# Modulation weights read in pieces of 256 rows by 512 columns, with their partial sums over 512 columns on VectorE alone

## The chip, the core and the metric

The kernel runs on one core of one Trainium2 chip. The metric is device time in microseconds (us), the median of several executions. Most executions of one kernel agree within 0.3%.

## The reference

One inference step of a four-layer network over 512 sample tokens and 128 prompt tokens, 1024 wide, all in float32. Every layer first makes its modulation vectors, normalises and modulates the tokens, runs a mixer of its kind (differential attention, retention, HGRN2, differential attention again), and adds the gated result to the tokens:

```
for l in range(DEPTH):                                   # 4 layers, kinds 0, 1, 2, 0
    sh_p, sc_p, ga_p = modulation(c_ctx[None, :], w_mod[l], b_mod[l])   # silu(c) @ w_mod[l] + b_mod[l],
    sh_s, sc_s, ga_s = modulation(c, w_mod[l], b_mod[l])                # cut into three parts of 1024
    hp = rms_norm(xp, g_pre[l]) * (1.0 + sc_p) + sh_p
    hs = rms_norm(xs, g_pre[l]) * (1.0 + sc_s) + sh_s
    yp, ys = mixer(hp), mixer(hs)                        # x @ w_in, the mixer, @ w_out
    xp = xp + ga_p * rms_norm(yp, g_post[l])
    xs = xs + ga_s * rms_norm(ys, g_post[l])
```

The change is in the product `silu(c) @ w_mod[l]`: a matrix of 1024 rows by 3072 columns per layer, against two vectors (the sample's c and the prompt's c_ctx). No value of the result is computed differently, apart from the order of the sums.

## The kernel before

**Work on TensorE.** All large products (x @ w_in, y @ w_out) are made of matmuls in fp32r, three for each product: the weights and the tokens are each cut into a high part (`whi`, `hh`) and a low part (`wlo`, `hl`). ScalarE makes the high part, VectorE (at line 116) the low part as a difference. TensorE's order is written out by hand (`manual_schedule`), by generators that `weave` interleaves: the projections of the next head fill the gaps of the mixer of this head. The order on VectorE, ScalarE, GpSimd and the DMA queue of SyncE (SP) is made by a scheduler that takes an instruction when its operands are ready by its own reckoning, so work that stands late in the program can be put into an earlier stage.

**The start** (`start`, lines 1270 to 1368). The first layer's shift and scale are made by TensorE, 128 columns at a time. Step k of 8: a product with `mraw` (line 1296), a copy `row` to SBUF (line 1298), a transposition on TensorE (line 1303), a reduction `mcol` (line 1305) and two small operations that write `modT` (lines 1306 and 1308). With `modT` the tokens, transposed on TensorE (line 1313), become `h` (line 1316), `hh` and `hl`, and then the first projection uses them (lines 1325 to 1327). All of it but TensorE's part, `hh` and `whi` runs on VectorE, in one queue.

**The other modulation vectors** are made off TensorE. `mod_load` fetches a piece of w_mod of 512 rows by 256 columns into `mraw` (two buffers) as 4 groups of 128 rows. `mod_next` is called after each unit of the projections with a number of groups (`mod_pace`). For a group and each of the two vectors it takes mraw times a column of silu(c) (`smod`) and adds it to `macc`, at line 371 on VectorE, 256 columns at once; for the first group, and in the two attention layers for every second group, ScalarE makes the product (line 369, into `mpart` for the latter, which VectorE adds over 512 values at line 373). `mpart` lies in the attention layer's own pool (`mod_pool`), so it can't be written before the stage ahead has given up that memory. After 8 groups the sums over rows still lie across the 128 partitions; `mod_turn` transposes them on TensorE (line 339, 4 of 128x128) and VectorE reduces them into `modT` (line 343). The table `MOD_IN` says which blocks of columns are made during which layer: 12 blocks of 256 in layer 0, 24 in layer 1, none in layer 2, 4 in layer 3.

**A boundary of two layers** (`out_layer`, lines 601 to 629). For each of five tiles of 128 tokens: y @ w_out, a norm, and the new tokens `xt` (line 619, VectorE). `pre` takes the sum of squares (line 408, ScalarE), `ms` (line 394, VectorE), `rs` (line 401, GpSimd) and the scaled tokens `xh` (line 410, ScalarE); `turn` transposes `xh` on TensorE (line 419) and makes `h` in two steps (lines 421 and 422, VectorE), `hh` (line 446, ScalarE) and `hl` (line 116, GpSimd for three of the tiles). The next layer's first products (`step`) use them. The chain xt, ms, rs, xh of the last tile is followed by a transposition at a fixed place in TensorE's order.

Of the kernel before, what the change touches and what calls it, by code (L numbers as in the profile page):

```python
# [11 lines left out]
F32 = mybir.dt.float32  # L12
# [3 lines left out]
AF = mybir.ActivationFunctionType  # L16
# [5 lines left out]
P = 128  # L22
# [15 lines left out]
         ("g", 3), ("qk", 7))  # L38
RW = (3.5, 9.0, 11.0, 0.5)
PACE = (155.0, 245.0, 195.0)  # L40
MOD_IN = (((0, range(8, 12)), (1, range(8))), ((1, range(8, 12)), (2, range(8)), (2, range(8, 12)), (3, range(8))), (),
          ((3, range(8, 12)),))
TOK = (0, 128, 384, 512, 256)


# [43 lines left out]
class Net:  # L89
    def __init__(self, ctx, tc, t):  # L90
        self.ctx, self.tc, self.nc, self.t = ctx, tc, tc.nc, t
        pool = lambda name, **kw: ctx.enter_context(tc.tile_pool(name=name, **kw))
        self.cp = pool("cp", bufs=1)
        self.wp = pool("wp", bufs=2)
        self.mp = pool("mp", bufs=1)
        self.dp = pool("dp", bufs=1, space=DRAM)
        self.pp = pool("pp", bufs=1, space=PSUM)
        self.mods, self.modr, self.modp = {}, [], None
        self.mod_owed, self.mod_row = 0, 0
        self.held = None  # L100

# [217 lines left out]
    def mod_load(self):  # L319

        if self.modq:
            l, b, i = self.modq.pop(0)
            raw = self.wp.tile([P, 4, 256], F32, tag="mraw", bufs=2, name="mraw")
            self.nc.sync.dma_start(raw, self.t["w_mod"][l, i * 512:i * 512 + 512, b * 256:b * 256 + 256].rearrange("(k p) n -> p k n", p=P))
            self.modr.append((l, b, i, raw))

    def mod_turn(self):

        nc = self.nc
        if self.modp is None:  # L330
            return
        l, b, acc = self.modp
        self.modp = None
        if b == 0:
            self.mods[l] = self.cp.tile([P, 24, 2], F32, tag="modT", bufs=3, name="modT")
        ps = self.one([P, 2, 2, P])
        for c in range(2):
            for j in range(2):
                nc.tensor.transpose(ps[:, c, j, :], acc[:, j, c * 128:c * 128 + 128], self.ident)
        r = slice(2 * b, 2 * b + 2)  # L340
        m = self.mods[l][:, r, :]
        wide = lambda a: a.unsqueeze(2).to_broadcast([P, 2, 2])
        nc.vector.tensor_reduce(out=m, in_=ps, axis=AX.X, op=ALU.add)
        nc.vector.tensor_tensor(out=m, in0=m, in1=wide(self.bmodT[:, l, r]), op=ALU.add)
        if 4 <= b < 8:
            nc.vector.tensor_scalar(out=m, in0=m, scalar1=1.0, scalar2=None, op0=ALU.add)
        if b >= 4:
            g = (self.gpre if b < 8 else self.gpost)[:, l, b % 4 * 2:b % 4 * 2 + 2]
            nc.vector.tensor_tensor(out=m, in0=m, in1=wide(g), op=ALU.mult)

    def mod_next(self, rows):

        nc = self.nc
        self.mod_owed += rows
        while self.mod_owed >= 1 and self.modr:
            self.mod_owed -= 1
            l, b, i, raw = self.modr[0]
            k = self.mod_row
            first = i == k == 0
            if first:  # L360
                self.macc = self.mp.tile([P, 2, 256], F32, tag="macc", bufs=2, name="macc")
            part = self.macc if first else None
            pool = self.mod_pool if k % 2 else None
            if pool is not None:
                part = pool.tile([P, 2, 256], F32, tag="mpart", bufs=2, name="mpart")
            for j in range(2):
                m, c = self.macc[:, j, :], self.smod[:, 4 * i + k, j:j + 1]
                if part is not None:
                    nc.scalar.activation(part[:, j, :], raw[:, k, :], AF.Copy, scale=c)
                else:  # L370
                    nc.vector.scalar_tensor_tensor(out=m, in0=raw[:, k, :], scalar=c, in1=m, op0=ALU.mult, op1=ALU.add)  # L371
            if pool is not None:
                nc.vector.tensor_tensor(out=self.macc, in0=self.macc, in1=part, op=ALU.add)
            if 4 * i + k == 5:
                self.mod_turn()
            self.mod_row = (k + 1) % 4
            if k == 3:
                self.modr.pop(0)
                if i == 1:
                    self.modp = (l, b, self.macc)  # L380
                self.mod_load()

    def mod_finish(self):
        self.mod_next(200)
        self.mod_turn()
        self.mod_owed = 0

# [268 lines left out]
    def diff(self, l, y):  # L656
        nc, tc, t = self.nc, self.tc, self.t
        j = SLOTS[l]
        lam_init = 0.8 - 0.6 * math.exp(-0.3 * l)
        with tc.tile_pool(name=f"da{l}", bufs=2, reuse_waits="tile") as mp:  # L660
            cc = self.const(mp, "ropec")
            cs = self.const(mp, "ropes")
            lv = mp.tile([P, 256], F32, tag="t1", name="lv")
            nc.sync.dma_start(lv, t["da_lambda"][j].rearrange("a b -> (a b)").partition_broadcast(P))
            self.gain = self.gains[:, 1 + j:2 + j]
            lp = mp.tile([P, 2, 64], F32, tag="sh", name="lp")
            lw = lv.rearrange("p (a b c) -> p a b c", a=2, b=2)
            nc.vector.tensor_tensor(out=lp, in0=lw[:, :, 0, :], in1=lw[:, :, 1, :], op=ALU.mult)
            ls = mp.tile([P, 2], F32, bufs=1, name="ls")
            nc.vector.tensor_reduce(out=ls, in_=lp, axis=AX.X, op=ALU.add)  # L670
            nc.scalar.activation(ls, ls, AF.Exp)
            nlam = mp.tile([P, 1], F32, bufs=1, name="nlam")
            nc.vector.tensor_tensor(out=nlam, in0=ls[:, 1:2], in1=ls[:, 0:1], op=ALU.subtract)
            nc.vector.tensor_scalar(out=nlam, in0=nlam, scalar1=-lam_init, scalar2=None, op0=ALU.add)
            st = types.SimpleNamespace(mp=mp, l=l, j=j, cc=cc, cs=cs, nlam=nlam, v={}, sg={}, q={}, k={})
            st.o, st.scored, st.done = {}, -1, -1
            self.mod_pool = mp
            for part in (("vg", 0), ("qk", 0)):
                for _ in self.diff_part(st, *part):
                    pass  # L680
            self.weave(self.diff_mix(st, y), self.stream(st, l, y, ORDER, self.diff_part, 4), 1.0, 1.0)
# [695 lines left out]
    def layers(self, depth):  # L1377
        nc, tc, t = self.nc, self.tc, self.t
        self.hh = self.cp.tile([P, KT, 640], F32R, name="hh")
        self.hl = self.cp.tile([P, KT, 640], F32R, name="hl")  # L1380
        xs, xp = t["x_sample"][0], t["x_prompt"][0]
        src = [xs[i * 128:i * 128 + 128, :] for i in range(4)] + [xp]
        ys, yp = t["y_sample"][0], t["y_prompt"][0]
        dst = [ys[i * 128:i * 128 + 128, :] for i in range(4)] + [yp]
        self.w_in = {0: t["da_w_in"], 1: t["ret_w_in"], 2: t["hg_w_in"]}
        self.w_out = {0: t["da_w_out"], 1: t["ret_w_out"], 2: t["hg_w_out"]}
        self.modq = []
        self.todo = sum((self.pieces(l) for l in range(depth)), [])
        self.raws, self.cuts, self.live, self.ahead = [], [], 0, False
        self.start(src)  # L1390
        self.x_in = src
        for l in range(depth):
            kind = KINDS[l]
            if l == depth - 1:
                self.x_out = dst
            else:
                self.x_out = [self.dp.tile([P, D], F32, tag=f"x{l}_{tt}", name=f"x{l}_{tt}") for tt in range(NT)]
            for m, bs in MOD_IN[l]:
                if m < depth:
                    self.modq += [(m, b, i) for b in bs for i in range(2)]  # L1400
            self.mod_pace, self.mod_pool = 4 * (len(self.modq) + len(self.modr)) / PACE[kind], None
            if not self.modr:
                self.mod_load()
                self.mod_load()
            if kind == 1:
                self.y_dram = self.dp.tile([P, NT, D], F32, name="y_dram")
            with tc.tile_pool(name=f"y{l}", bufs=1, reuse_waits="tile") as yp_:
                y = yp_.tile([P, NT, D], F32, name="y")
                (self.diff, self.ret, self.hg)[kind](l, y)
                self.out_layer(l, y)  # L1410
            self.x_in = self.x_out
# [32 lines left out]
```

## Time and profile before

| | |
|---|---|
| median of 3 executions | 1883.51 us (1880.94 to 1884.3) |
| the profiled execution: its own time, its span | 1883.0 us, 1881.2 us |
| TensorE (matmuls) | 1803.2 us busy, 96% of the span |
| VectorE | 1307.0 us busy, 69% |
| ScalarE | 981.3 us busy, 52% |
| GpSimd | 301.3 us busy, 16% |
| mean granted TensorE clock | 0.992 of full speed |

The span is the time from the first to the last instruction; the 1.8 us around it belong to the execution's own time. Busy time is the time in which at least one instruction of the engine runs. The granted clock is the share of TensorE's full speed that it was given over a stretch.

### The profile page before, as it was taken

The numbers are of one execution on the slowest core, as the hardware profiler recorded it, in microseconds if no ns is written. First come the engines' busy times: TensorE is split into PE (matmuls) and PEld (weight loads), VectorE is DVE, ScalarE is ACT, GpSimd is POOL, SyncE is SP. The second block draws the span as 40 slices with busy tenths as digits, with TensorE's granted clock in tenths as the row PEclk, the third lists the DMA queues.
The fourth block names the chain that finished last, engine by engine and source line by source line (L and its number), as shares of the span: only waits on it lengthen the run. The fifth ranks groups of instructions, "written<-read, shape, count | busy, mean of one in ns | idle before, by whom it ended". The sixth has DMA issues, their size and how long they took to land.

```text
span 1881.2 us, 31937 instructions
## 1 busy us (share of the span) xinstructions
PE 1803.2 (96%) x12060; PEld 1648.3 (88%) x12060; DVE 1307.0 (69%) x2681; ACT 981.3 (52%) x2271; POOL 301.3 (16%) x249
## 2 busy tenths in 40 slices
PE   6999999999999999999999999999979999999998
PEld 4889999977888888889878899999968889999976
DVE  4768888847788898873335666676774766767654
ACT  3556666645544444443333366666664645655552
POOL 0000000003222223222101223332331300000001
PEclk9999999999999999999999999999989999999999
DMA  9645455414354445443323322222214463443322
GB/s 302 181 122 151 146 146 166 122 51 157 117 160 146 149 150 158 124 135 101 115 93 101 96 71 66 63 63 74 62 43 135 140 171 91 116 114 100 100 73 101
DMA packets 231536, 224.39 MB, mean 119 GB/s; under 512 B 11619, under 2 KB 201558, under 8 KB 231382
## 3 DMA queue, kind: packets, MB, share of 16 engines
q1 hardware_dynamic: 230912, 221.96, 39.4%
q8 instruction: 95, 1.56, 0.4%
q14 instruction: 59, 0.48, 0.1%
q10 hardware_dynamic: 470, 0.39, 0.1%
HBM read 174.59 MB, written 18.35 MB: 103 GB/s over the span
## 4 chain that ended last, share of the span: by engine, by line
PE 62%; DVE 17%; ACT 8%; DMA 5%; issue 4%; POOL 2%; SPq 1%; DVEq 0%; ACTq 0%; POOLq 0%
PE one L474 6%; PE one L476 6%; PE one L475 6%; PE one L250 5%; PE one L251 5%; PE one L252 5%; DVE macc L371 3%; PE one L830 3%; PE one L225 3%; PE one L226 3%; PE one L227 3%; DVE wlo L116 2%; PE two L792 2%; PE two L793 2%; ACT whi L178 1%
## 5 line engine op out<-in xcount | busy, mean ns | idle before, releaser
L250 PE MATMUL one<-hh,whi 128*128 128x320 f32 x1152 | 364.6, 316 | 3.3 <-ACT qp L769 1.8
L252 PE MATMUL one<-hh,wlo 128*128 128x320 f32 x1152 | 356.1, 309 | 0.1
L251 PE MATMUL one<-hl,whi 128*128 128x320 f32 x1152 | 356.2, 309 | 0.0
L116 DVE TENSOR_TENSOR wlo<-raw,whi 128x1024 fp32r<-128x1024 f32 x192 | 235.8, 1234 | 142.6 <-ACT whi L178 142.1
L474 PE MATMUL one<-whi,hh 128*128 128x512 f32 x744 | 301.1, 405 | 6.5 <-ACT yo L569 3.2
L476 PE MATMUL one<-whi,hl 128*128 128x512 f32 x744 | 293.6, 395 | 1.7 <-DVE ms L394 1.3
L475 PE MATMUL one<-wlo,hh 128*128 128x512 f32 x744 | 292.2, 393 | 0.0
L178 ACT ACTIVATE whi<-raw 128x1024 fp32r<-128x1024 f32 x192 | 201.5, 1056 | 155.3 <-PE one L251 58.4
L250 PEld LDWEIGHTS one<-hh,whi 128*128 128x128 f32 x1152 | 216.9, 188 | 5.3 <-ACT qp L769 2.2
L251 PEld LDWEIGHTS one<-hl,whi 128*128 128x128 f32 x1152 | 217.1, 188 | 0.5
L252 PEld LDWEIGHTS one<-hh,wlo 128*128 128x128 f32 x1152 | 216.9, 188 | 0.4 <-DVE wlo L116 0.4
L401 POOL TENSOR_TENSOR rs<-ms,mhalf 128x1 f32<-128x1 f32 (+1 forms) x72 | 65.6, 913 | 901.3 <-DVE ms L399 724.8
L371 DVE SCALAR_TENSOR_TENSOR macc<-mraw,smod,macc 128x256 f32<-128x256 f32 x432 | 209.1, 527 | 0.2
L225 PE MATMUL one<-whi,hh 128*128 128x256 f32 x720 | 207.5, 288 | 0.0
L226 PE MATMUL one<-wlo,hh 128*128 128x256 f32 x720 | 200.8, 279 | 0.0
L227 PE MATMUL one<-whi,hl 128*128 128x256 f32 x720 | 200.8, 279 | 0.0
L474 PEld LDWEIGHTS one<-whi,hh 128*128 128x128 f32 x744 | 140.9, 189 | 36.9 <-DVE p L1017 4.0
L476 PEld LDWEIGHTS one<-whi,hl 128*128 128x128 f32 x744 | 140.5, 189 | 36.0 <-DVE hl L116 2.2
L475 PEld LDWEIGHTS one<-wlo,hh 128*128 128x128 f32 x744 | 140.9, 189 | 27.4
L225 PEld LDWEIGHTS one<-whi,hh 128*128 128x128 f32 x720 | 135.3, 188 | 1.5
L226 PEld LDWEIGHTS one<-wlo,hh 128*128 128x128 f32 x720 | 135.4, 188 | 0.0
L227 PEld LDWEIGHTS one<-whi,hl 128*128 128x128 f32 x720 | 135.0, 187 | 0.0
(345 smaller groups left out, 3548.6 us busy)
## 6 DMA issues: line engine op xcount, KB each, us to landing
mraw<-in_w_mod SPq DMA_DIRECT2D x96, 512.0 KB, 4.4
raw<-in_da_w_in SPq DMA_DIRECT2D x56, 512.0 KB, 4.5
raw<-in_hg_w_in SPq DMA_DIRECT2D x36, 512.0 KB, 3.9
raw<-in_ret_w_in SPq DMA_DIRECT2D x64, 256.0 KB, 3.1
kk<-ks SPq DMA_DIRECT2D x64, 160.0 KB, 2.8
kz<-ks SPq DMA_DIRECT2D x64, 160.0 KB, 2.8
qq<-q SPq DMA_DIRECT2D x64, 128.0 KB, 3.0
raw<-in_da_w_out SPq DMA_DIRECT2D x16, 512.0 KB, 3.4
```

What stands on the lines that cost most here:

```text
L116: return (eng or self.nc.gpsimd).tensor_tensor(out=out, in0=full, in1=hi.bitcast(F32), op=ALU.subtract)
L178: self.nc.scalar.activation(hi, raw, AF.Copy)
L225: mm(out, xh, wh[:, k % 4, :], start=(first and k == ks[0]), stop=False)
L226: mm(out, xh, wl[:, k % 4, :], start=False, stop=False)
L227: mm(out, xl, wh[:, k % 4, :], start=False, stop=(last and k == ks[-1]))
L250: nc.tensor.matmul(ps, wh[:, k, :], self.hh[:, k, c], start=(k == 0), stop=False)
L251: nc.tensor.matmul(ps, wh[:, k, :], self.hl[:, k, c], start=False, stop=False)
L252: nc.tensor.matmul(ps, wl[:, k, :], self.hh[:, k, c], start=False, stop=(k == KT - 1))
L371: nc.vector.scalar_tensor_tensor(out=m, in0=raw[:, k, :], scalar=c, in1=m, op0=ALU.mult, op1=ALU.add)
L474: mm(ps, xh, wh, start=(first and k == ks[0]), stop=False)
L475: mm(ps, xh, wl, start=False, stop=False)
L476: mm(ps, xl, wh, start=False, stop=(last and k == ks[-1]))
```

## The change

A piece is now 256 rows by 512 columns (2 groups of 128 rows; the same 512 KB). One step is now one instruction: one group for one of the two vectors, over 512 columns. The first group's product is made by ScalarE, every other step is one instruction on VectorE, in every layer; `mpart`, its pool and the addition at line 373 are gone. A block of 512 columns is turned in two halves, during the fifth and the seventh group of the next block. The pace in steps is as before (4 a piece, the same number of pieces).

```diff
-MOD_IN = (((0, range(8, 12)), (1, range(8))), ((1, range(8, 12)), (2, range(8)), (2, range(8, 12)), (3, range(8))), (),
-          ((3, range(8, 12)),))
+MOD_IN = (((0, range(4, 6)), (1, range(4))), ((1, range(4, 6)), (2, range(4)), (2, range(4, 6)), (3, range(4))), (),
+          ((3, range(4, 6)),))
...
-            raw = self.wp.tile([P, 4, 256], F32, tag="mraw", bufs=2, name="mraw")
-            self.nc.sync.dma_start(raw, self.t["w_mod"][l, i * 512:i * 512 + 512, b * 256:b * 256 + 256].rearrange("(k p) n -> p k n", p=P))
+            raw = self.wp.tile([P, 2, 512], F32, tag="mraw", bufs=2, name="mraw")
+            self.nc.sync.dma_start(raw, self.t["w_mod"][l, i * 256:i * 256 + 256, b * 512:b * 512 + 512].rearrange("(k p) n -> p k n", p=P))
...
             l, b, i, raw = self.modr[0]
-            k = self.mod_row
-            first = i == k == 0
-            if first:
-                self.macc = self.mp.tile([P, 2, 256], F32, tag="macc", bufs=2, name="macc")
-            part = self.macc if first else None
-            pool = self.mod_pool if k % 2 else None
-            if pool is not None:
-                part = pool.tile([P, 2, 256], F32, tag="mpart", bufs=2, name="mpart")
-            for j in range(2):
-                m, c = self.macc[:, j, :], self.smod[:, 4 * i + k, j:j + 1]
-                if part is not None:
-                    nc.scalar.activation(part[:, j, :], raw[:, k, :], AF.Copy, scale=c)
-                else:
-                    nc.vector.scalar_tensor_tensor(out=m, in0=raw[:, k, :], scalar=c, in1=m, op0=ALU.mult, op1=ALU.add)
-            if pool is not None:
-                nc.vector.tensor_tensor(out=self.macc, in0=self.macc, in1=part, op=ALU.add)
-            if 4 * i + k == 5:
+            k, j = divmod(self.mod_row, 2)
+            r = 2 * i + k
+            if r == j == 0:
+                self.macc = self.mp.tile([P, 2, 512], F32, tag="macc", bufs=2, name="macc")
+            m, c = self.macc[:, j, :], self.smod[:, r, j:j + 1]
+            if r == 0:
+                nc.scalar.activation(m, raw[:, k, :], AF.Copy, scale=c)
+            else:
+                nc.vector.scalar_tensor_tensor(out=m, in0=raw[:, k, :], scalar=c, in1=m, op0=ALU.mult, op1=ALU.add)
+            if j == 1 and r in (4, 6):
                 self.mod_turn()
-            self.mod_row = (k + 1) % 4
-            if k == 3:
+            self.mod_row = (self.mod_row + 1) % 4
+            if k == j == 1:
                 self.modr.pop(0)
-                if i == 1:
-                    self.modp = (l, b, self.macc)
+                if i == 3:
+                    self.modp = [(l, b, half, self.macc) for half in range(2)]
                 self.mod_load()
...
-            self.mod_pool = mp
...
-                    self.modq += [(m, b, i) for b in bs for i in range(2)]
-            self.mod_pace, self.mod_pool = 4 * (len(self.modq) + len(self.modr)) / PACE[kind], None
+                    self.modq += [(m, b, i) for b in bs for i in range(4)]
+            self.mod_pace = 4 * (len(self.modq) + len(self.modr)) / PACE[kind]
```

The program has 80 loads of a piece and 160 transpositions at line 339 (340 after) on either side; TensorE has the same instructions, of which only the place of these transpositions moves. On VectorE 432 steps over 256 columns and 64 additions become 280 steps over 512 columns (line 367 after), on ScalarE 208 products over 256 columns become 40 over 512.

The scheduler's order moves as well. **The first place is in VectorE's queue during the start**, from the `row` of step k = 6 to that of the last of the eight, k = 7 (`row`, `mcol`, `modT`, `h`, `hl` as told above). Before:

```order
L1298 COPY row<-two 128x256
L116 TENSOR_TENSOR wlo<-raw,whi 128x1024
L1305 TENSOR_REDUCE mcol<-two 128x4
L1306 SCALAR_TENSOR_TENSOR modT<-mcol,b_105,par 128x2
L1308 TENSOR_SCALAR modT<-mcol,par 128x2
L1316 TENSOR_SCALAR h<-two,modT 128x2x256
L1316 TENSOR_SCALAR h<-two,modT 128x128
L116 TENSOR_TENSOR hl<-h,hh 128x640
L1298 COPY row<-two 128x256
```

And after, from the same `row` to the same `row`:

```order
L1292 COPY row<-two 128x256
L367 SCALAR_TENSOR_TENSOR macc<-mraw,smod,macc 128x512
L116 TENSOR_TENSOR hl<-h,hh 128x640
L367 SCALAR_TENSOR_TENSOR macc<-mraw,smod,macc 128x512
L116 TENSOR_TENSOR wlo<-raw,whi 128x1024
L1299 TENSOR_REDUCE mcol<-two 128x4
L367 SCALAR_TENSOR_TENSOR macc<-mraw,smod,macc 128x512 x4
L1300 SCALAR_TENSOR_TENSOR modT<-mcol,b_105,par 128x2
L1302 TENSOR_SCALAR modT<-mcol,par 128x2
L1292 COPY row<-two 128x256
```

Before, VectorE's first step of these sums (line 373) stands behind the last `hl` of the start; after, 21 steps stand ahead of that `hl`: 6 before the `row` of step k = 5, and 15 from there on. A further 7 follow before the first rope of the attention. On the SP queue the loads of pieces move along: six more stand ahead of the tables `c_ropec` and `c_ropes`.

**The second place is in VectorE's queue at the boundary of layers 2 and 3**, from the last tile's second half of y (line 553, 548 after) on. Before:

```order
L553 TENSOR_TENSOR xh<-one,gb 128x512
L421 TENSOR_TENSOR h_15699<-two,modT 128x1024
L394 TENSOR_SCALAR ms<-ss 128x1
L422 TENSOR_TENSOR h_15699<-h_15699,modT 128x1024
L619 SCALAR_TENSOR_TENSOR xt<-xh,rs,xt 128x1024
L421 TENSOR_TENSOR h_15738<-two,modT 128x1024
L394 TENSOR_SCALAR ms<-sx 128x1
```

After:

```order
L548 TENSOR_TENSOR xh<-one,gb 128x512
L416 TENSOR_TENSOR h_15297<-two,modT 128x1024
L367 SCALAR_TENSOR_TENSOR macc<-mraw,smod,macc 128x512
L389 TENSOR_SCALAR ms<-ss 128x1
L367 SCALAR_TENSOR_TENSOR macc<-mraw,smod,macc 128x512
L417 TENSOR_TENSOR h_15297<-h_15297,modT 128x1024
L367 SCALAR_TENSOR_TENSOR macc<-mraw,smod,macc 128x512 x2
L614 SCALAR_TENSOR_TENSOR xt<-xh,rs,xt 128x1024
L367 SCALAR_TENSOR_TENSOR macc<-mraw,smod,macc 128x512 x2
L416 TENSOR_TENSOR h_15336<-two,modT 128x1024
L367 SCALAR_TENSOR_TENSOR macc<-mraw,smod,macc 128x512
L389 TENSOR_SCALAR ms<-sx 128x1
```

Seven steps of the sums for layer 3 now stand between these operations of the last tile; before, the first of them stood behind the boundary. At the boundary of layers 0 and 1 the order after is the same, operation for operation; there the order before had steps of 256 columns among them too, as the rows below show with their times.

## Rows read from the trace of the kernel before

**Rows 1.** The page, part 1: TensorE's busy time, share and instructions.

```profile
PE 1803.2 (96%) x12060; PEld 1648.3 (88%) x12060; DVE 1307.0 (69%) x2681; ACT 981.3 (52%) x2271; POOL 301.3 (16%) x249
```

**Rows 2.** Busy time by stretch: length, PE, PEld, DVE, ACT, POOL (instructions), clock, DMA.

```profile
33.20:66.60 33.40, 31.57 (x203) 22.61 (x202) 21.05 (x44) 11.90 (x17) 0.00 (x0) 0.95 0.73 197
...
49.00:66.60 17.60, 17.60 (x103) 13.22 (x102) 12.45 (x26) 6.88 (x10) 0.00 (x0) 0.90 0.36 100
...
100.00:110.00 10.00, 8.48 (x49) 8.15 (x50) 8.07 (x21) 5.51 (x15) 0.00 (x0) 0.83 0.55 146
...
470.00:475.00 5.00, 3.42 (x14) 2.88 (x15) 4.13 (x7) 2.90 (x4) 2.72 (x2) 0.75 0.34 103
475.00:480.00 5.00, 5.00 (x21) 4.07 (x20) 5.00 (x10) 1.81 (x4) 0.00 (x0) 0.90 0.08 18
...
480.00:830.00 350.00, 342.65 (x1990) 305.00 (x1990) 298.85 (x670) 154.78 (x344) 94.58 (x69) 1.00 0.48 148
```

**Rows 3.** Groups of instructions: count, busy us, mean ns of one, idle before.

```profile
L371 DVE SCALAR_TENSOR_TENSOR macc<-mraw,smod,macc 128x256 f32<-128x256 f32 x432 | 209.1, 527 | 0.2
...
L373 DVE TENSOR_TENSOR macc<-macc,mpart 128x512 f32<-128x512 f32 x64 | 43.8, 686 | 0.6 <-ACT mpart L369 0.3
...
L872 DVE SCALAR_TENSOR_TENSOR pe<-pe,rc 128x640 f32<-128x640 f32 x64 | 56.5, 882 | 1.2
```

**Rows 4.** VectorE in time: start, duration of the merged instructions, what, count.

```profile
65.11 0.82 DVE L116 TENSOR_TENSOR hl<-h,hh 128x640 fp32r<-128x640 f32 x1
...
66.56 0.88 DVE L371 SCALAR_TENSOR_TENSOR macc<-mraw,smod,macc 128x256 f32<-128x256 f32 x2
```

**Rows 5.** TensorE in time: start, duration, instruction, in brackets its wait.

```profile
48.74 0.33 PE L1303 MATMUL two<-c_ident,row 128*128 128x128 f32 x1 [1.83 <-DVE row L1298]
...
85.58 0.41 PE L250 MATMUL one<-hh,whi 128*128 128x320 f32 x1 [1.27 <-ACT qp L769]
...
100.40 0.58 PE L792 MATMUL two<-kk,qq 128*128 128x320 f32 x1 [2.23 <-DMA raw<-in_da_w_in]
...
471.58 0.33 PE L419 MATMUL two<-c_ident,xh 128*128 128x128 f32 x1 [3.50 <-ACT xh L410]
...
1482.17 0.38 PE L419 MATMUL two<-c_ident,xh 128*128 128x128 f32 x2
```

**Rows 6.** Boundary of layers 0 and 1: VectorE, then GpSimd, in time.

```profile
458.58 2.16 DVE L371 SCALAR_TENSOR_TENSOR macc<-mraw,smod,macc 128x256 f32<-128x256 f32 x2
...
461.80 0.87 DVE L371 SCALAR_TENSOR_TENSOR macc<-mraw,smod,macc 128x256 f32<-128x256 f32 x2
...
463.79 3.03 DVE L371 SCALAR_TENSOR_TENSOR macc<-mraw,smod,macc 128x256 f32<-128x256 f32 x2
...
467.87 0.87 DVE L371 SCALAR_TENSOR_TENSOR macc<-mraw,smod,macc 128x256 f32<-128x256 f32 x2
468.66 0.14 DVE L394 TENSOR_SCALAR ms<-sx 128x1 f32<-128x1 f32 x1
...
457.65 2.41 POOL L116 TENSOR_TENSOR hl<-h,hh 128x1024 fp32r<-128x1024 f32 x1 [0.56 <-ACT hh L446]
...
463.05 3.08 POOL L116 TENSOR_TENSOR hl<-h,hh 128x1024 fp32r<-128x1024 f32 x1 [2.31 <-ACT hh L446]
```

**Rows 7.** Boundary of layers 2 and 3: VectorE, GpSimd, ScalarE, in time.

```profile
1472.36 0.14 DVE L394 TENSOR_SCALAR ms<-ss 128x1 f32<-128x1 f32 x1
1472.47 2.90 DVE L422 TENSOR_TENSOR h<-h,modT 128x1024 f32<-128x1024 f32 x1
1475.81 1.28 DVE L619 SCALAR_TENSOR_TENSOR xt<-xh,rs,xt 128x1024 f32<-128x1024 f32 x1 [0.43 <-POOL rs L401]
...
1478.31 0.15 DVE L394 TENSOR_SCALAR ms<-sx 128x1 f32<-128x1 f32 x1
...
1471.89 2.40 POOL L116 TENSOR_TENSOR hl<-h,hh 128x1024 fp32r<-128x1024 f32 x1 [0.56 <-ACT hh L446]
...
1480.89 1.15 ACT L410 ACTIVATE xh<-xt,rs 128x1024 f32<-128x1024 f32 x1 [2.61 <-POOL rs L401]
```

More of the change, by code (lines that the diff above doesn't have):

```diff
@@ L97, in __init__ @@
         self.pp = pool("pp", bufs=1, space=PSUM)
-        self.mods, self.modr, self.modp = {}, [], None
+        self.mods, self.modr, self.modp = {}, [], []
         self.mod_owed, self.mod_row = 0, 0
@@ L329, in mod_turn @@
         nc = self.nc
-        if self.modp is None:
+        if not self.modp:
             return
-        l, b, acc = self.modp
-        self.modp = None
-        if b == 0:
+        l, b, half, acc = self.modp.pop(0)
+        if b == half == 0:
             self.mods[l] = self.cp.tile([P, 24, 2], F32, tag="modT", bufs=3, name="modT")
@@ L338, in mod_turn @@
             for j in range(2):
-                nc.tensor.transpose(ps[:, c, j, :], acc[:, j, c * 128:c * 128 + 128], self.ident)
-        r = slice(2 * b, 2 * b + 2)
+                o = half * 256 + c * 128
+                nc.tensor.transpose(ps[:, c, j, :], acc[:, j, o:o + 128], self.ident)
+        o = 2 * half + 4 * (b % 2)
+        r = slice(8 * (b // 2) + o, 8 * (b // 2) + o + 2)
         m = self.mods[l][:, r, :]
@@ L344, in mod_turn @@
         nc.vector.tensor_tensor(out=m, in0=m, in1=wide(self.bmodT[:, l, r]), op=ALU.add)
-        if 4 <= b < 8:
+        if b // 2 == 1:
             nc.vector.tensor_scalar(out=m, in0=m, scalar1=1.0, scalar2=None, op0=ALU.add)
-        if b >= 4:
-            g = (self.gpre if b < 8 else self.gpost)[:, l, b % 4 * 2:b % 4 * 2 + 2]
+        if b // 2:
+            g = (self.gpre if b // 2 == 1 else self.gpost)[:, l, o:o + 2]
             nc.vector.tensor_tensor(out=m, in0=m, in1=wide(g), op=ALU.mult)
@@ L384, in mod_finish @@
         self.mod_next(200)
+        self.mod_turn()
         self.mod_turn()
```

## The prediction

> **What bounds the kernel.** I read the busy times first. TensorE is busy for 1803.2 of 1881.2 us [rows 1], so its order never has to get shorter for the time to fall; only its 78 us of idle time and the stretches at a low clock can move. The change leaves TensorE's instructions as they are. So I looked, stretch by stretch, at where TensorE waits for VectorE, ScalarE or a load, since these are the engines whose work the change makes shorter and moves. Over the table of stretches and TensorE's rows in time [rows 2, 5] four places matter: the start (TensorE 31.57 of 33.40 us busy, clock 0.95), the first heads of layer 0 (two waits, 85.58 and 100.40, and a clock of 0.83 behind the second), the boundary of layers 0 and 1 (a wait of 3.50), and the retention layer, where 7.35 of 350 us are idle. The boundary of layers 2 and 3 has no wait: the transposition at 1482.17 starts with none behind it [rows 5].
>
> **What the work costs.** On VectorE 432 steps of 256 columns and 64 additions of 512 [rows 3] give way to 280 steps of 512. Their means (527 and 686 ns) hold overlap with the next instruction and waits; back to back, two steps of 256 take 0.88 us from the first start to the second end [rows 4], so one takes about 0.40 us of the queue and ends 0.08 after the next starts. Together before: 209.1 + 43.8 = 252.9 us [rows 3]. No row shows the fused step at 512 columns. From below it costs more than the 0.40 at 256; from above no more than 0.80, the 882 ns at 640 columns of the same operation at line 872 [rows 3] less that 0.08. On the line between the two, 256/384 of the way, it is 0.40 + 0.67 x 0.40 = 0.67; the plain addition over 512 columns has 686 ns, 0.61 less overlap. I take 0.66 us. 280 x 0.66 = 185 us: VectorE gets some 68 us lighter and ScalarE loses most of its products. Neither engine is the bound, so this counts only where TensorE waits.
>
> **Term 1, the start.** Up to `hl`'s end at 65.93 [rows 4] VectorE's queue now holds 21 steps, 13.9 us; in 33.20:66.60 it was idle for 33.40 - 21.05 = 12.35 us [rows 2], so they do not fit whole. Of them 6 (4.0 us) stand ahead of the `row` of step k = 5, where VectorE was idle for 15.8 - 8.6 = 7.2 us (first row of the stretches less the second): they fit, and TensorE's wait of 1.83 us for a `row` at 48.74 [rows 5] may grow a little. From 49.00 on VectorE has 12.45 us of old work, of which 0.7 lies behind the `hl`, and 15 new steps of 9.9 us: 49.0 + 11.75 + 9.9 = 70.7 if it never waits. The first projection is held by this `hl`: +4.8 us. If all idle time were usable, only 13.9 - 12.35 = 1.5 would be lost; if VectorE also waits for ScalarE's `hh` and for loads on the way, up to 8. I take +4.8, and +1 for a clock that was 0.90 from 49.00 on and will stay low for the longer wait.
>
> [...]
>
> **Term 2, what layer 0 gives back.** The wait at 85.58 (1.27) is for a copy on ScalarE and the one at 100.40 (2.23) for copies whose weight load does not move with TensorE [rows 5]. When TensorE arrives some 5 us later, both should be gone, and with the second one the clock of 0.83 in 100:110: 10 x 0.17 = 1.7 us [rows 2]. 1.27 + 2.23 + 1.7 = -5.2. Terms 1 and 2 together: 4.8 + 1 - 5.2 = **+0.6**, with -2 (nothing lost at the start, part given back) and +5.8 (nothing given back) as ends.
>
> **Term 3, the boundary of layers 0 and 1.** Before, eight steps of 256 columns lie in the last tile's chain from 458.58 to 468.66 [rows 6], 8 x 0.40 = 3.2 us; after, seven of 512 stand there, 4.6. The wait of 3.50 grows by 1.4: **+1.4** (-1 to +3).
>
> The rows show a second thing: two steps that lie beside GpSimd's `hl` take 2.16 and 3.03 us instead of 0.87, and end when that `hl` ends (460.06, 466.13) [rows 6]; `h` at 1472.47 takes 2.90 likewise [rows 7]. So a step that falls into an `hl` of GpSimd waits for it. [...]
>
> **Term 4, the retention layer.** In 480:830 TensorE is idle for 7.35 us [rows 2]. VectorE had 24 blocks of 14 steps of 0.40 there, 134 us, and will have 12 blocks of 14 of 0.66, 111; it was 85% busy and gets to some 79%. Nothing says which of the idle time is VectorE's; I take a fifth, **-1.5** (0 to -7).
>
> **Term 5, the boundary of layers 2 and 3.** Before, no step stands there, and `xh` ends at 1480.89 + 1.15 = 1482.04, just before TensorE needs it at 1482.17 [rows 5, 7]: the slack is 0.1 us. After, seven steps stand in the last tile's chain. Replayed on the rows: the first starts at 1472.4, under GpSimd's `hl` (1471.89 to 1474.29), and ends about 1474.3; `ms`, one step and `h` (1.2) follow to 1476.3, two steps to 1477.6, `xt` (1.28) to 1478.9 instead of 1477.1; GpSimd's next `hl` (3.1 as at 463.05 [rows 6], from about 1477.5, behind ScalarE's `hh`) then holds the next of two steps to 1480.6, the other ends at 1481.3; `h` and one more step end at 1483.1, where `ms` starts (was 1478.31). At the other boundary 471.58 - 468.66 = 2.92 us lie between the same `ms` and the transposition [rows 5, 6]: 1486.0 here, 3.8 late. The other bound is the same chain at the other boundary: 3.50 [rows 5] and the 1.4 of term 3, 4.9. Between them I take 4.3. TensorE stands still meanwhile, and at the other boundary such a halt was followed by a clock of 0.75 and 0.90 over 5 us each [rows 2], 1.25 + 0.5 = 1.7 us. **+6.0** (0 to +7).
>
> Behind `ms` nothing else of layer 3 waits longer: the steps left over are ahead of their due time. ScalarE's fewer products and the 80 loads of the same size I cost at nothing, since TensorE does not wait for either outside the places above; were the loads late, the steps, not the chain, would be late.
>
> **The sum.** 0.6 + 1.4 - 1.5 + 6.0 = +6.5 on the profiled execution's own 1883.0: 1889.5. The median of the runs is 0.5 above that execution, so I forecast **1890 us**.
>
> **Rivals.** *No change*: the seven steps at the boundary of layers 2 and 3 cost little, because they issue ahead of the `hl`s and GpSimd waits instead, whose results are not due as soon; then I put term 5 at 1.5, term 3 at 0.5, and the time at 1883.5 + 0.6 + 0.5 - 1.5 + 1.5 = 1884.6. For it: VectorE had 0.43 us to spare at `xt`, and 1.7 of `h`'s 2.90 were such a hold already. Against: 4.6 us of new work stand in one queue with a slack of 0.1. *Faster*: VectorE's 68 us are what the retention layer waited for; the 7.35 us shrink to about 1 (-6), the start fits (-2), and only term 3 is paid (+1.4): about 1877. It decides if the idle time in 480:830 falls below 3 us and the transposition at the boundary of layers 2 and 3 does not wait. Against it: VectorE is not full in that stretch. *Much slower*: the start's 5.8 is not given back, since loads and copies move with TensorE: 1890 + 5.2 - 0.5 = about 1895.
>
> **How the numbers follow.** My forecast has 0.60 (1886.5 to 1893), no change 0.24, faster 0.10, much slower 0.06. A difference of 0.2%, 3.8 us, is about what a measurement of this kernel tells from none. The forecast and the much slower case both lie above 1887.3. Faster 0.10, same 0.24, slower 0.66. The range leaves out the faster case and part of the last: 1881.5 to 1896.5; the lower end is the no-change case with the start at its lower bound.
>
> **What would show it.** Right: the step of 512 columns at a mean of 0.70 to 0.80 us; the start's last `hl` near 71; no waits at the places of 85.58 and 100.40; seven steps in the last tile's chain at the boundary of layers 2 and 3, a wait of 3.8 to 4.9 us on its transposition and a clock below 1 behind it. Wrong: that transposition without a wait (term 5 falls, and the time with it to about 1884), the two waits of layer 0 still there (terms 1 and 2 add up to over 5), or 3 us and less idle in the retention layer (term 4 is the larger one).

## The result

The changed kernel is slower: 1916.93 us (median of 4 executions, 1914.66 to 1919.95) against 1883.24 us (4 executions), a ratio of 1.018 (95% interval 1.0168 to 1.0192), or 33.7 us. Slower was forecast, but 6.5 us of it.

The page of the kernel after, parts 1 and 5: busy time, share of the span and instructions of each engine; then the group of the new step with count, busy us, mean ns and idle time before it.

```profile
PE 1810.6 (94%) x12060; PEld 1657.2 (86%) x12060; DVE 1283.2 (67%) x2465; ACT 924.6 (48%) x2103; POOL 293.1 (15%) x249
...
L367 DVE SCALAR_TENSOR_TENSOR macc<-mraw,smod,macc 128x512 f32<-128x512 f32 x280 | 215.1, 800 | 17.1 <-DMA mraw<-in_w_mod 15.5
```

VectorE and ScalarE are both less busy than before and the kernel is longer all the same [rows 1]. TensorE runs the same products on both sides, in the same order but for the transpositions of the sums. So the two traces can be paired instruction by instruction, and the lag of each kernel behind the one before read at any place. Here at eleven, for all kernels of this study (us; positive is later; the names are those of the experiments below; one profiled execution each). The six kernels that have the changed kernel's start stand at 5.8 to 7.1 at 67, so differences of 1 us say little:

```
time in the kernel before  67   144   365   464   500   850   910  1450  1490  1545   end
after                     6.6  -1.0  20.1  20.1  22.9  19.0  21.8  25.1  33.1  36.0  35.5
e1_turn_2_4               6.7  -1.2   0.4   0.4   3.1   1.5   4.0   5.7  14.3  17.2  16.8
e2_turn_0_2               6.4  -0.6   1.6   1.7   4.8  16.6  19.4  21.6  30.2  32.1  31.5
e3_held                  -1.2   3.9  26.9  26.5  29.7  25.6  28.1  31.0  30.6  39.5  39.2
e4_share                 -0.3   5.4  22.4  22.2  25.6  20.6  23.4  26.8  26.7  32.3  31.8
e5_small_pieces           2.6  -4.1  -1.3  -1.5  -1.4   1.0   1.1   1.3   4.6   4.0   4.7
e6_light_layer            5.8  -1.4  -0.2  -0.2   3.1   1.0   3.9   9.8   9.5   7.3   5.0
e7_light_and_held         6.4  -1.1   0.8   1.2  -4.5   3.8   6.4  14.1  13.8  12.0   9.2
e8_before_held            0.3  -0.4  -0.4  -0.3  -6.0  -4.1  -4.1  -0.8  -1.2  -0.5  -3.3
e9_thin                   7.1  -0.6   0.5   0.2   3.4  -0.9   1.1   2.6  11.2  12.8  12.9
e10_before_layer1_held   -0.1  -1.5  -1.5  -1.1  -6.8  -5.0  -4.9  -3.4  -3.5  -3.4  -3.4
```

The start is lost and given back, as forecast. Then comes what no term of the prediction holds: **21 us between 144 and 365, in the body of layer 0**. The boundary of layers 2 and 3 (1450 to 1490) costs 8.0, layer 3's first heads 2.9, the boundary of layers 0 and 1 2.8, the end of layer 1 (850 to 910) 2.8; the retention layer gives 3.9 back.

Layer 0 by stretch (length, then busy time and instructions of PE, PEld, DVE, ACT, POOL, then the granted clock), before and after, over the same instructions of TensorE but for a few:

```profile
140.00:370.00 230.00, 229.12 (x1773) 225.31 (x1771) 196.50 (x478) 153.37 (x431) 6.94 (x6) 1.00 0.50 145
```

```profile
139.00:390.00 251.00, 233.58 (x1771) 229.56 (x1770) 193.12 (x443) 124.15 (x351) 7.02 (x6) 0.98 0.45 126
```

TensorE's idle time goes from 0.9 to 17.4 us, though VectorE has 3.4 us less to do there, and its busy time, for the same work, from 229.12 to 233.58 us; the 16.5 and the 4.5 us make the 21. What TensorE waits for, by the waits in that stretch of the kernel after (us in total, times, longest), and one of them in time:

```profile
PE one L814 <- DVE pe L866: 13.7, 5, 6.2
PE one L824 <- ACT at L817: 2.8, 3, 2.3
PE one L339 <- ACT qp L763: 0.8, 1, 0.8
```

```profile
191.05 1.30 PE L814 MATMUL one<-c_ident,pe 128*128 128x128 f32 x5 [6.17 <-DVE pe L866]
...
236.19 0.74 PE L814 MATMUL one<-c_ident,pe 128*128 128x128 f32 x5 [1.66 <-DVE pe L866]
```

`pe` is the attention's weights (line 866, VectorE), which TensorE transposes. Before, the same waits came to 0.5 us in that stretch. Why `pe` is late stands in VectorE's queue. First VectorE by 10 us in the kernel before, over most of one cycle of two heads (some 42 us); then the kernel after, in time: TensorE's transposition of a finished block of sums (it stands at line 339 in both kernels), ScalarE's first product of the next block, and VectorE up to the `pe` at 235.16.

```profile
180.00:190.00 10.00, 9.88 (x72) 9.62 (x71) 10.00 (x29) 6.61 (x21) 1.17 (x1) 1.00 0.57 167
190.00:200.00 10.00, 10.00 (x78) 9.97 (x77) 9.90 (x27) 7.38 (x22) 0.00 (x0) 1.00 0.66 186
200.00:210.00 10.00, 10.00 (x86) 9.75 (x85) 8.07 (x20) 6.70 (x21) 0.00 (x0) 1.00 0.59 166
210.00:220.00 10.00, 10.00 (x86) 10.00 (x85) 5.46 (x13) 6.01 (x16) 0.00 (x0) 1.00 0.16 52
```

```profile
222.14 0.60 PE L339 MATMUL one<-c_ident,macc 128*128 128x128 f32 x4
...
222.83 1.33 ACT L365 ACTIVATE macc<-mraw,smod 128x512 f32<-128x512 f32 x2
...
224.19 0.75 DVE L367 SCALAR_TENSOR_TENSOR macc<-mraw,smod,macc 128x512 f32<-128x512 f32 x1
...
225.58 0.74 DVE L367 SCALAR_TENSOR_TENSOR macc<-mraw,smod,macc 128x512 f32<-128x512 f32 x1
...
226.31 0.75 DVE L367 SCALAR_TENSOR_TENSOR macc<-mraw,smod,macc 128x512 f32<-128x512 f32 x1
226.97 1.22 DVE L116 TENSOR_TENSOR wlo<-raw,whi 128x1024 fp32r<-128x1024 f32 x1
228.11 0.75 DVE L367 SCALAR_TENSOR_TENSOR macc<-mraw,smod,macc 128x512 f32<-128x512 f32 x1
...
235.16 0.89 DVE L866 SCALAR_TENSOR_TENSOR pe<-pe,rc 128x640 f32<-128x640 f32 x1
```

VectorE's cycle has a part in which its queue is full (10.00 and 9.90 of 10 us) and a part in which it is half empty (5.46); in the next three cycles three of four such stretches have 9.4 us or more and the fourth 3.9 to 5.9. In the full part TensorE waits for next to nothing, but there is no room either. A block of sums has two buffers of `macc`; the next block's first product follows the transposition that frees one by 0.1 us, and its 14 steps (the bunch) follow it, one or two at a time between the chain's own operations, until all are done some 21 to 22 us later. After, this happens every 46 to 52 us, 14 steps of 0.66 us (9.2 us of the queue) at a time, and at each of its four times in layer 0 at the front of the full part. Before, it happened every 21 us with 6 steps of 0.40 and 4 additions of 0.61 (4.8 us), so each half of the cycle had one. None of VectorE's waits for a load of a piece (15.5 us in all, in the group above) lies in this stretch, so late loads are not the cause.

### The profile page after: what moved, and what is told of

It reads as the page before. It is cut to its first block, busy times and chain, and to the rows that moved or that the text cites. A ratio compares the mean times of both kernels' runs of the same rounds, so it can differ in the third digit from the quotient of the medians.

```text
span 1916.7 us, 31501 instructions
## 1 busy us (share of the span) xinstructions
PE 1810.6 (94%) x12060; PEld 1657.2 (86%) x12060; DVE 1283.2 (67%) x2465; ACT 924.6 (48%) x2103; POOL 293.1 (15%) x249
## 4 chain that ended last, share of the span: by engine, by line
PE 61%; DVE 18%; DMA 7%; ACT 7%; issue 4%; POOL 2%; SPq 2%; DVEq 0%; POOLq 0%; ACTq 0%
PE one L469 7%; PE one L471 7%; PE one L470 7%; PE one L250 5%; PE one L251 5%; PE one L252 5%; DVE macc L367 4%; PE one L225 3%; PE one L824 3%; PE one L226 3%; PE one L227 3%; DVE wlo L116 2%; DMA mraw<-in_w_mod 2%; PE two L786 1%; PE one L814 1%
## 5 line engine op out<-in xcount | busy, mean ns | idle before, releaser
L367 DVE SCALAR_TENSOR_TENSOR macc<-mraw,smod,macc 128x512 f32<-128x512 f32 x280 | 215.1, 800 | 17.1 <-DMA mraw<-in_w_mod 15.5
L471 PEld LDWEIGHTS one<-whi,hl 128*128 128x128 f32 x744 | 141.2, 190 | 34.7 <-DVE hl L443 1.3
L790 ACT ACTIVATE pe<-two,nm 128x640 f32<-128x640 f32 x128 | 101.2, 793 | 78.7 <-DVE nm L788 78.5
```

Source lines behind the costliest of these rows:

```text
L471: mm(ps, xl, wh, start=False, stop=(last and k == ks[-1]))
```

## The experiments

**The place of the bunch.** Two kernels differ from the changed one in one line, which has (2, 4) in e1 and (0, 2) in e2.

```diff
-            if j == 1 and r in (4, 6):
+            if j == 1 and r in (2, 4):
                 self.mod_turn()
```

> The changed kernel with one number changed: the finished block is turned during the third and fifth group of the next block instead of the fifth and seventh, so that TensorE's transpositions, which free a buffer of macc, stand some 10 us earlier in TensorE's order. Theory A (the 14 steps of a block run in one bunch right behind the second transposition of the block before, and in layer 0 this bunch falls each time into the half of the 40 us cycle of two heads in which VectorE is already full): the bunches move into the other half, of the 22 us lost in layer 0 at least 15 come back, the waits for pe at line 814 fall from 14.3 us to under 4, and the time is 1895 to 1902. Rival B (the step of 512 columns is too long for the chain of a head wherever it stands, or VectorE's load without ScalarE's share is what counts): within 5 us of 1917.

> The changed kernel with the turns during the first and third group, some 20 us earlier than in the changed kernel. Theory A: the bunches then run half in the full and half in the light part of the cycle, so the time lies between that of the turns at three and five and that of the changed kernel, 1900 to 1912. Rival B: 1912 to 1922, as any other place of the turns.

With (2, 4): 1898.67 us, 18 less than the changed kernel. Layer 0's loss is gone, with the same steps on VectorE. Its stretch, and VectorE and ScalarE behind the transposition at 202.56:

```profile
139.00:371.00 232.00, 229.34 (x1774) 225.80 (x1774) 193.85 (x443) 124.19 (x352) 7.02 (x6) 1.00 0.48 137
```

```profile
202.56 0.60 PE L339 MATMUL one<-c_ident,macc 128*128 128x128 f32 x4
...
203.20 1.34 ACT L365 ACTIVATE macc<-mraw,smod 128x512 f32<-128x512 f32 x2 [1.23 <-PE one L339]
...
203.96 0.75 DVE L367 SCALAR_TENSOR_TENSOR macc<-mraw,smod,macc 128x512 f32<-128x512 f32 x1
...
213.80 1.40 DVE L367 SCALAR_TENSOR_TENSOR macc<-mraw,smod,macc 128x512 f32<-128x512 f32 x2
```

The first product waits for the transposition by name (1.23 us), and the 14 steps are done in 11 us in the light part. No wait of TensorE for `pe` is left in the stretch. Theory A holds, rival B falls.

With (0, 2): 1910.03 us, inside what was expected, but for another reason. Layer 0 loses only 2.2 us between 144 and 365, though half of the bunch lies in the full part: it starts at 196.0, behind the third of the cycle's four `pe` (195.3), where the changed kernel's starts at 172.5, ahead of the first (190.0). So it seems to count what of the full part is still due behind the bunch, not how much of the bunch lies in it. The loss is in the retention layer instead, 11.8 us between 500 and 850, where TensorE waits for a VectorE product of a head (two lines of the waits in 632 to 760; over 500 to 870 the two come to 7.2 and 4.8 us, in the changed kernel to 0.5 and 1.5):

```profile
PE one L469 <- DVE p L1011: 6.7, 3, 2.6
PE one L925 <- DVE kl L116: 3.0, 2, 1.7
```

So the place that is best in one layer need not be so in the next; why this one is bad there was not tried.

**The length of the bunch.** In this kernel part of the work is left out, as its expectation says.

```diff
-            else:
+            elif r % 2 == 0 or (l, b) not in ((1, 0), (1, 1), (1, 2), (1, 3)):
                 nc.vector.scalar_tensor_tensor(out=m, in0=raw[:, k, :], scalar=c, in1=m, op0=ALU.mult, op1=ALU.add)
```

> The changed kernel with work left out: in the four blocks that layer 0 makes behind its first two, the odd groups are not added, so a bunch has 6 steps (4.0 us of VectorE's time) instead of 14 (9.2 us); turns, loads and everything else stay where they are. Theory A (a bunch at the front of the cycle's busy part delays the pe behind it by what it is longer than the 10 operations, 4.8 us, that stood there before; four bunches of 9.2 us cost some 20 of the 22 us): layer 0's loss falls to under 3 us and the time to 1894 to 1899. Rival G (it is the turns, eight transpositions and two reductions close together, or TensorE's order, and not VectorE's steps): at least 12 of the 22 us stay, 1905 to 1917.

1896.45 us; layer 0 loses 1.1 us instead of 21 (lags at 144 and 365). Loads, turns and ScalarE's products stayed where they were, so the loss is the steps' time in VectorE's queue: a bunch of 4.0 us fits where one of 9.2 does not. By the sum, four bunches that are each 9.2 - 4.8 = 4.4 us longer than what stood in that part before make 17.6 us, near the 16.5 us by which TensorE's idle time grew. The other 4.5 us are busy time, the same products at a lower clock: in the changed kernel, in the stretch of the first long wait (6.17 us) and the one behind it, it is 0.86 and 0.82.

```profile
182.00:193.00 11.00, 4.83 (x29) 4.60 (x28) 11.00 (x28) 4.12 (x10) 1.18 (x1) 0.86 0.65 193
193.00:203.00 10.00, 10.00 (x62) 10.00 (x62) 6.63 (x16) 3.43 (x12) 0.00 (x0) 0.82 0.67 193
```

**ScalarE's share.** What was taken from ScalarE is given back, over 512 columns:

```diff
+            elif self.mod_pool is not None and k:
+                part = self.mod_pool.tile([P, 512], F32, tag="mpart", bufs=2, name="mpart")
+                nc.scalar.activation(part, raw[:, k, :], AF.Copy, scale=c)
+                nc.vector.tensor_tensor(out=m, in0=m, in1=part, op=ALU.add)
             else:
...
+            self.mod_pool = mp
```

> The changed kernel with ScalarE's share given back: in the attention layers every second group's product is made by ScalarE into mpart, in the attention layer's pool, and added by VectorE over 512 columns (0.61 us instead of 0.66, so VectorE's load hardly changes). Theory A: the bunches hang on the same transpositions, so at least 12 of layer 0's 22 us stay; the start and the boundary of layers 2 and 3 are free of steps as in the run with the copy of smod: 1900 to 1910. Rival D (what kept the steps apart before was ScalarE making every second product): layer 0's loss is under 5 us and the time 1883 to 1893.

1912.22 us, 2 above the expected range: 17 us are still lost between 144 and 365. Rival D falls: it is not the engine that makes the product. A further 5.7 us are lost between 67 and 144 and 5.6 between 1490 and 1545, at the heads of the two attention layers, as in e3 below. The other way round, the kernel before with all steps on VectorE, but over 256 columns:

```diff
-            pool = self.mod_pool if k % 2 else None
+            pool = None
```

> The kernel before with one line changed: every step of the sums on VectorE, still over 256 columns (no product of ScalarE but the first, no mpart). A turn then frees a bunch of 14 x 0.40 = 5.6 us every 21 us, where the changed kernel has 14 x 0.66 = 9.2 us every 42 us; VectorE's load in layer 0 grows from some 58 to 67 us. Theory A (the length of a bunch and the half of the cycle it falls into decide): half of the bunches fall into the light half, layer 0 loses under 8 us; the steps are free to move ahead as in the changed kernel, so the boundary of layers 2 and 3 and layer 3's first heads lose 8 to 11: 1890 to 1900. Rival B (VectorE's load without ScalarE's products decides): layer 0 loses 22 us or more, 1908 to 1925.

1888.70 us (ratio 1.0027, interval 1.0016 to 1.0039), 1.3 below the expected range: the boundary of layers 2 and 3 and layer 3's first heads cost 2.7 us (1.3 to 4.0), not 8 to 11. VectorE is busy for 200.3 us of the stretch from 139 to 369, more than in the kernel before, yet only 2.8 us are lost between 144 and 365, after 4.1 had been won by 144. Rival B falls. So one part of the change, all on VectorE, costs some 5 us; the other, blocks of 512 columns, costs the rest.

**The head start.** To keep the steps of a layer out of the stage ahead, they read a copy of `smod` that lies in that layer's own pool:

```diff
+            self.sm = mp.tile([P, KT, 2], F32, bufs=1, name="sm")
+            nc.vector.tensor_copy(out=self.sm, in_=self.smod[:, :, 0:2])
...
-            m, c = self.macc[:, j, :], self.smod[:, r, j:j + 1]
+            m, c = self.macc[:, j, :], (self.smod if self.sm is None else self.sm)[:, r, j:j + 1]
```

> The changed kernel, with the steps of the two attention layers reading a copy of smod that lies in the attention layer's own pool, so that none of them can be put ahead of that layer: none stands in the start's chain, none in the chain of the last tile at the boundary of layers 2 and 3. Theory A: the boundary gives back its 8 us (5.8 of wait, 2.2 of clock), the start gave its 6.6 back already and changes nothing; layer 0 still loses its 22, as the bunches hang on the transpositions: 1905 to 1911. Rival C (the head start of 28 steps during the start is what shifts the bunches into the full stretches): layer 0 loses under 8 us and the time is under 1897.

1923.57 us: neither theory had that, though layer 0 still loses its 22 (23.0), as theory A has it, and rival C falls. The edit did what it says: the start loses nothing (lag -1.2 at 67 instead of 6.6), and the transposition at the boundary of layers 2 and 3 no longer waits (31.0, then 30.6). But the 28 steps that could run ahead then run at the head of the layers, and cost 5.1 us between 67 and 144 and 8.9 between 1490 and 1545. TensorE's longest waits in 60 to 115, and what ScalarE's `kp` waits for, a VectorE operation:

```profile
PE one L250 <- ACT kp L765: 5.2, 1, 5.2
ACT kp L765 <- DVE sh L764: 5.3, 3, 3.5
PE two L788 <- DMA qq<-q: 1.8, 1, 1.8
```

In the changed kernel they ran in the start, and the loss there was all given back. Here the gate did not cure the bunch; it only let it fall elsewhere.

**A light layer, and the boundary of layers 0 and 1.** The next two kernels have the turns at (2, 4), the two blocks for layer 3 in layer 2, and the copy in layer 2's pool; e7 also has it in layer 1's pool. e8 has both edits in the kernel before.

```diff
-MOD_IN = (((0, range(4, 6)), (1, range(4))), ((1, range(4, 6)), (2, range(4)), (2, range(4, 6)), (3, range(4))), (),
-          ((3, range(4, 6)),))
+MOD_IN = (((0, range(4, 6)), (1, range(4))), ((1, range(4, 6)), (2, range(4)), (2, range(4, 6)), (3, range(4))), ((3, range(4, 6)),),
+          ())
```

> The turns at the third and fifth group as in the first experiment, and the two blocks for layer 3 made in layer 2 (where VectorE is 20 to 70 per cent busy) instead of layer 3, their steps reading a copy of smod in layer 2's own pool, so that they can't stand at the boundary of layers 1 and 2. Theory A (28 steps in one bunch cost where VectorE's chain is what TensorE waits for, and nothing where it is light): the 8 us at the boundary of layers 2 and 3 and the 3 of layer 3's first heads go, nothing new comes in layer 2: 1885 to 1890. Rival F (28 free steps cost some 8 us at the head of any layer, as with the copy of smod in layers 0 and 3): 1894 to 1900.

> The same, and layer 1's steps too read a copy of smod in layer 1's own pool, so that none stands in the chain of the last tile at the boundary of layers 0 and 1 either (seven do in the changed kernel, eight of 256 columns in the kernel before). Theory A: the wait of that transposition (6.1 us in the changed kernel, 3.5 before) and the 1.7 us of clock behind it go, so some 5 us less than the run without this copy: 1880 to 1886. Rival F: the bunch moves into the first units of the retention layer, where VectorE is over 80 per cent busy, and costs as much there: no difference to that run within 2 us.

> The kernel before (256 columns, ScalarE's share) with the same two edits: the blocks for layer 3 made in layer 2, and the steps of layers 1 and 2 reading a copy of smod in their own pool. Theory A: no steps in the chain at the boundary of layers 0 and 1, so the wait of 3.5 us and 1.7 us of clock go; the boundary of layers 2 and 3 had none: 1876 to 1880 against 1881 to 1884 before. If this is as fast as the run with pieces of 512 columns and both edits or faster, the wider pieces are worth nothing here. Rival F: 1881 to 1885.

e6: 1890.12 us, 8.5 less than e1 (by the ratios to the kernel before, 1.0031 and 1.0089, 11 us less) and 0.1 above theory A's range; nothing is lost at 1450 to 1545 any more (9.8 to 7.3), though 5.9 us come in layer 2 (3.9 to 9.8), against 1.7 there in e1, so the light layer is not free. e7: 1890.35 us, above theory A's 1886 and no difference to e6, as rival F has it. The boundary is won (1.2 to -4.5 where e6 has -0.2 to 3.1), and lost again in the retention layer's first units, in one wait:

```profile
PE one L925 <- DVE p L1013: 8.0, 1, 8.0
```

e8: 1878.73 us, ratio 0.9974 (0.9963 to 0.9984), inside theory A's range and 11.6 us below e7: the wider pieces are worth nothing here. With steps of 256 columns the same edit wins 5.7 us at the boundary and gives back only 1.9 behind it. Then one edit alone (the `sm` of e3, made in layer 1's own pool, in the kernel before):

> The kernel before with one edit: only layer 1's steps read a copy of smod in layer 1's own pool (layer 3's blocks stay in layer 3). Theory A: the wait of 3.5 us at the boundary of layers 0 and 1 and the 1.7 us of low clock behind it go and about 2 come back in the retention layer, as in the run with both edits at that place: -3.5 to -4.5, 1879 to 1881 where before is 1883.5. Rival (the run with both edits won its time in layer 3): within 1.5 us of before.

1878.16 us, 0.8 below the expected range, ratio 0.9972 (0.9961 to 0.9983), some 5 us: as fast as with both edits, and **faster than both kernels**. The transposition at the boundary, after a gap of 3.50 us before [rows 5], follows the product ahead of it without one, and the clock stays at 1.00:

```profile
466.54 0.40 PE L476 MATMUL one<-whi,hl 128*128 128x512 f32 x1
466.77 1.04 PE L419 MATMUL two<-c_ident,xh 128*128 128x128 f32 x8
...
465.00:470.00 5.00, 5.00 (x28) 4.20 (x27) 2.05 (x2) 0.93 (x1) 2.38 (x1) 1.00 0.19 53
```

## Why the prediction was wrong

**The step that failed** is the one that priced the steps outside the named places at nothing: "VectorE gets some 68 us lighter and ScalarE loses most of its products. Neither engine is the bound, so this counts only where TensorE waits." TensorE hardly waited in 144 to 365 before (0.9 us idle), so no term stood there. But no wait is not slack: VectorE's queue was full for half of each cycle and more. The runs showed 21 us of loss there in place of nothing. A sum over the layer hides this (196.50 of 230 us, 85%, rows above); 10 us stretches show it. I also never asked what decides when a step may run. With two buffers of `macc` it is the transposition of the block before last, so a block of 512 columns makes one bunch of 9.2 us where two of 256 made two, of 4.8 us each (5.6 without ScalarE's share). The other places of the bunch (e1, e2) and the thinned bunch (e9) show that both its place and its length count; none of the rivals had it.

**The sum of the places that were priced** came out near the forecast: -1.0 + 2.8 - 3.9 + 8.0 = +5.9 us by the lags, against +6.5. That is luck in part: the two boundaries cost 3.4 us more than priced, the start and the retention layer 4.0 less. The rest of the 35.5 us stands where no term stood: 21.1 in layer 0, 2.8 at the end of layer 1, 3.3 between 910 and 1450, 2.9 in layer 3's first heads (where "nothing else of layer 3 waits longer" was wrong), and -0.5 behind them.

**The step's price** was right: 0.66 us was taken; two steps run in 1.41 us and one in 0.74, so 0.67 from start to start. What that saves was not: the "68 us lighter" sets 252.9 us of busy time, overlap and waits included, against 280 times a start-to-start price. With 0.40 and 0.61 for the old steps and additions it would have been 212 - 185 = 27 us; VectorE's busy time fell by 23.8 (1307.0 to 1283.2).

**Terms 1 and 2, the start**: +5.8 and -5.2 were forecast, +6.6 and -7.6 came. The last `hl` ends at 73.2 (forecast near 71, upper bound 73.9), the waits at the places of 85.58 and 100.40 are gone, and the clock that was 0.83 is 1.00:

```profile
72.36 0.83 DVE L116 TENSOR_TENSOR hl<-h,hh 128x640 fp32r<-128x640 f32 x1
...
100.00:110.00 10.00, 9.99 (x71) 9.53 (x70) 8.91 (x21) 5.00 (x13) 0.00 (x0) 1.00 0.72 204
```

Where the further 2.4 us of the gain come from was not followed. What I had not seen is why leaving the steps out of the start would be worse: e3 pays for the same steps in the first heads.

**Term 3** was +1.4, measured 2.8: the wait at the boundary of layers 0 and 1 is 6.09 us instead of 3.50. The steps' own time was priced, but here too the `xt` of the last tile now falls under GpSimd's `hl` (it starts at 484.16), as told under term 5:

```profile
484.24 3.43 DVE L614 SCALAR_TENSOR_TENSOR xt<-xh,rs,xt 128x1024 f32<-128x1024 f32 x1
...
494.29 1.97 PE L414 MATMUL two<-c_ident,xh 128*128 128x128 f32 x8 [6.09 <-ACT xh L405]
```

**Term 4** was -1.5, measured -3.9. It was priced from VectorE's load alone; with the turns at (2, 4) the same stretch gives only 1.6 back (e1), at (0, 2) it loses 11.8 (e2), so the place of the turns counts there as well. The cause of the larger gain was not tried.

**Term 5** was right in mechanism and too small: +6.0 forecast, 8.0 measured, a wait of 6.09 where 4.3 was taken. e3 shows that it is the seven steps: without them there is no wait. VectorE and GpSimd at that boundary, the transposition, and two stretches with the clock:

```profile
1496.99 2.92 DVE L367 SCALAR_TENSOR_TENSOR macc<-mraw,smod,macc 128x512 f32<-128x512 f32 x1
...
1503.02 3.43 DVE L614 SCALAR_TENSOR_TENSOR xt<-xh,rs,xt 128x1024 f32<-128x1024 f32 x1
1506.37 1.40 DVE L367 SCALAR_TENSOR_TENSOR macc<-mraw,smod,macc 128x512 f32<-128x512 f32 x2
...
1509.49 0.14 DVE L389 TENSOR_SCALAR ms<-sx 128x1 f32<-128x1 f32 x1
...
1502.95 2.42 POOL L116 TENSOR_TENSOR hl<-h,hh 128x1024 fp32r<-128x1024 f32 x1 [1.91 <-ACT hh L441]
...
1513.06 1.33 PE L414 MATMUL two<-c_ident,xh 128*128 128x128 f32 x5 [6.09 <-ACT xh L405]
...
1510.00:1515.00 5.00, 1.94 (x9) 1.94 (x10) 3.41 (x5) 2.10 (x2) 2.79 (x2) 0.58 0.34 100
1515.00:1520.00 5.00, 5.00 (x18) 3.99 (x17) 4.87 (x6) 2.49 (x4) 1.39 (x1) 0.74 0.18 70
```

I let GpSimd's second `hl` fall on a step; it fell on `xt`, which began 0.07 us behind it and took 3.43 us instead of 1.28 [rows 7]. `ms` to transposition took 3.57 us, not 2.92. (The steps of rows 6 that were held ran on for 0.3 us behind their `hl`, and the second of each pair followed; they do not end with it, as the prediction reads.) The clock fell to 0.58 and 0.74, lower than at the other boundary before.

**What stays open.** The end of layer 1 (2.8 us): the eight kernels with blocks of 512 columns lose 2.0 to 2.9 there, the three with 256 lose 0.0 to 0.1. The last block of 512 is turned in two halves at one place, which may be the cause; that was not tried. In 910 to 1450, where the changed kernel has no steps, the lag grows by 3.3 us in it, 1.7 in e1, 1.5 in e10 and 0.2 in e5. This was not followed.

## What to carry to other kernels

Work that only has to be done some time is placed by what lets it start: if that is a buffer, its size sets how much runs in one bunch, and the instruction that frees it sets where. Read the busy time of the engine that gets the work in stretches shorter than the loop's cycle, not per layer: an engine at 85% can be full for half of each cycle and more, and nobody waits for it until something is added in front of the result that is due. Taking such work out of a critical chain with a gate pays only if the place that it falls to has room for it, as the same edit with steps of 256 and of 512 columns shows.

## What was not expected of the hardware

A hold by GpSimd's `hl` fell on the VectorE instruction with two operands in SBUF that started behind it, and at the boundary of layers 2 and 3 that was the one that was due, `xt`, by 0.07 us. Two that started just behind an `hl` of GpSimd and read two operands in SBUF were held until it ended: a step at 1496.99 (2.92 us instead of 0.74; `hl` from 1496.96, 2.41 long) and `xt` at 1503.02 (3.43 instead of 1.28). GpSimd had started first both times, by 0.03 and 0.07 us. In the kernel before, VectorE had started first at two places, and there the `hl` took longer, as the no-change rival has it: `xt` ran from 462.59 to 463.86, and the `hl` that began at 463.05 took 3.08 us [rows 6] instead of 2.41; `xt` ran from 1475.81 to 1477.09 [rows 7], and the `hl` that began at 1476.55 took 2.82. An `h` that reads `two`, which lies in PSUM, was not held: 1.23 us at 1483.32, under the `hl` that ran from 1483.07 to 1485.50.

```profile
462.59 1.27 DVE L619 SCALAR_TENSOR_TENSOR xt<-xh,rs,xt 128x1024 f32<-128x1024 f32 x1
...
1483.32 1.23 DVE L421 TENSOR_TENSOR h<-two,modT 128x1024 f32<-128x1024 f32 x1 [2.87 <-PE two L419]
...
1476.55 2.82 POOL L116 TENSOR_TENSOR hl<-h,hh 128x1024 fp32r<-128x1024 f32 x1 [0.78 <-ACT hh L446]
...
1483.07 2.43 POOL L116 TENSOR_TENSOR hl<-h,hh 128x1024 fp32r<-128x1024 f32 x1 [2.21 <-ACT hh L446]
```
